# One layer of a neighbourhood-attention, retention and gated-MLP network on one core: sums of activation blocks by adding DMA transfers, and four edits to the order of weights, stores and finishes

## The chip, the core and the metric

The kernel runs on one core of one Trainium2 chip. A core has five engines with an instruction queue each: TensorE (PE in the profile, its weight loads PEld), VectorE (DVE), ScalarE (ACT), GpSimd (POOL) and SyncE (SP), which here only issues DMA transfers. SyncE, ScalarE and GpSimd have DMA queues of their own (SPq, ACTq, POOLq in the profile). The metric is the time of one launch in microseconds on the device, as the median of several runs.

## The reference

One layer over 1024 latent tokens of width 1024 on a grid of 16 x 64, with 256 context tokens, in fp32. Cut to what matters:

```python
hx = modulate(rmsnorm(x), sh1, sc1);  hc = modulate(rmsnorm(ctx), csh1, csc1)
q, k, v, rq, rk, rv, rg, ga, gb = split(hx @ w_in)        # and the same of hc
o_na  = neighbourhood_attention(q, k, v, context keys and values)    # 8 heads of 64
o_ret = layernorm(bidirectional_retention(rope(rq), rope(rk), rv)) * silu(rg)   # 4 heads, 128 -> 256
x = x + g1 * ((sigmoid(ga) * (o_na @ w_proj_na) + sigmoid(gb) * (o_ret @ w_proj_ret)) @ w_out)
h = modulate(rmsnorm(x), sh2, sc2)
u = conv3(h @ w_up) + conv_b                              # depthwise over tokens, d_ff = 2816
a, val = split(u)
x = x + g2 * ((silu(a) * val) @ w_down)
return rmsnorm(x) * final_g
```

## The kernel before

**Products.** Every fp32 product is made of three TensorE passes on a reduced fp32 type. Each operand is split in a high part, a copy by ScalarE (L88), and a low part, the source minus the high part by VectorE (L89); the passes are high x high, high x low and low x high. So each loaded block passes one ScalarE and one VectorE instruction before TensorE can use it.

**Buffers of weights.** A weight block of 128 x 512 is loaded by SyncE's queue into a tile `raw` (three buffers, L93), and split into a tile of the common ring `wc` (`wtile()`, six buffers) or into a tile that the caller gives (`wload(..., into=t)`).

**Stages in the order of time.** Start (to about 98 us); neighbourhood attention with gate projections between its parts (to about 388); the four retention heads (to about 670); remaining gate projections (to about 721); the attention projection and the gates that use seven products for eight blocks (to about 1035); the output projection (to about 1130); the up stage with the convolution (to about 1543); the down stage (to about 1756); the last finishes.

**Retention.** `Head` (L1114) loads eight weight blocks of a head by key block kb. Blocks from KH = 4 on go into tiles `wx`, six buffers in the pool `rt` of this stage; blocks 0 to 3 go into the common ring. `front(i)` computes a chunk's projections from all eight blocks; the first two chunks are context (L123 to L125 with `hc`), the next ones latent (`hx`). `decay_masks` builds the decay tables from a table `dtab` loaded at L1104, on ScalarE (L1108, L1109) and VectorE. The computation of a chunk's output (`Mix`) follows one head later; `mix_c` (L1244 on) transposes an output block, copies it by ScalarE and stores it to `d_oret` by ScalarE's queue. For the last two blocks of the last head the copy goes into a tile `oe` in a `raw` buffer, the store is put in a list `stores`, and SyncE issues it after the attention rows have been loaded (L1383, L1384).

**Attention projection.** The attention rows `onr` are loaded, transposed in groups of four into six PSUM banks (`tpn`, L1388), and split from PSUM by ScalarE (L1390) and VectorE (L1391) into `ona`. Then come the products `pn`, each with a weight block `w_pna[db, 0]` (L1520).

**Up stage.** `Seven` (L1398) computes a 2 x 2 block product by seven products (Strassen in Winograd's form). Its sums of weights s1 to s4 are POOL instructions (L1405 to L1408). `Up.step(n)` does product n of one unit; 22 units run interleaved, about 19.7 us each. When all four results of a unit are there, `conv` (L1781) filters gate and value on ScalarE and VectorE (L1786 to L1788) and multiplies them (L1790) into `at`, whose two halves are the blocks A11, A21 (j below NH = 11) or A12, A22 (its partner j + NH). The units are ordered j, j + NH, j + 1, and so on, so every second unit completes a pair. Then `conv` stores A12 and A22, makes S1 = A21 - A22, S2 = S1 - A11, S3 = A11 - A21, S4 = A12 + S2 on POOL (L1804) in `raw` buffers, and stores each by SyncE, all in the DRAM tensor `d_a`.

**Sums by transfers.** Sums of weight blocks for the down stage are made in DRAM: `block_sums` (L549) copies blocks and adds others onto them by POOL-issued DMA transfers with an accumulating operation. `puts(it, src, n)` (L583) first copies a column of `src` on POOL, which makes POOL wait until `src` is written, and then issues the next n of these transfers. In the up stage this happens at products 1 and 3 of each unit after the first; what is left of the list is issued behind the last unit.

**Who sets the order.** A scheduler of the framework orders each engine's instructions by its own estimates. `late` (L536) pins an instruction behind everything written before it on its engine; it is used for the adding transfers. Inside `manual_schedule` the written order holds; the last four-pair block loop of the down stage (L2002 on) is such a region.

**Down stage.** `steps(p, ...)` (L1917 on) runs step p of seven: for each of 11 pairs j, `operands` takes the activation block and weight block named in `DOWN[p]` from a stream of loads that runs ahead (`ur`, twelve buffers), splits both (`ahl`, `wc`), and 12 matmuls add them to four banks, one for each of QB = 4 token blocks. Between the steps the banks are combined: `p1` (step 0), `u2` (L1959, step 1), `u3` (step 3), and so on. `finish(tb, dh)` (L1940 on) makes the final norm of a token block: two short POOL instructions for the root (L1942, L1943), one scaling each on ScalarE (L1945) and VectorE (L1946), two stores by SyncE.

```python
DOWN = (("A11", "B11"), ("S2", "T2"), ("A12", "B21"), ("S3", "T3"), ("S1", "T1"), ("A22", "T4"), ("S4", "B22"))
```

Of the kernel before, what the change touches and what calls it, by code (L numbers as in the profile page):

```python
# [8 lines left out]
F32 = mybir.dt.float32  # L9
F32R = mybir.dt.float32r  # L10
# [30 lines left out]
def tile_hybrid_layer(ctx, tc: tile.TileContext, io, dbg=None):  # L41
# [1072 lines left out]
    class Head:  # L1114
        def __init__(self, h):
            self.h = h
            fwd = h % 2 == 0
            self.order = list(range(NTB)) if fwd else list(range(NTB - 1, -1, -1))
            self.back = self.order[::-1]
            self.ci = 0 if fwd else 1  # L1120
            self.oi = 1 - self.ci
            self.wr = []
            for kb in range(KB):
                t = rt.tile([P, 2, 512], F32R, tag="wx", bufs=6, name="wx") if kb >= KH else None
                self.wr.append(wload(io["w_ret"][h, kb], into=t))
# [118 lines left out]
        def mix_c(self, n):  # L1244
# [4 lines left out]
            h = self.h  # L1249
            end = h == RH - 1 and n >= NTB - 2  # L1250
            if end:
                ot = wpool.tile([P, 512], F32, tag="raw", bufs=3, name="oe")[:, : 2 * P].rearrange("p (b t) -> p b t", b=2)
            else:
                ot = rt.tile([P, 2, P], F32, tag="ot", bufs=2, name="ot")
            act.copy(ot, tp)
            stores.append((d_oret[2 * h : 2 * h + 2, :, tb * P : (tb + 1) * P].rearrange("b p t -> p b t"), ot))
            if not end:
                act.dma_start(*stores.pop())

    stores = []  # L1260

# [73 lines left out]
    while not mix.done():  # L1335
        slot(pieces_of(tl, 2 if mix.n < NTB else 3), mix)
    for it in (tl, gate_sums):
        for _ in it:
            pass
# [39 lines left out]
    for n in range(KB):  # L1379
        raw = g_raw("onr")  # L1380
        sync.dma_start(raw, d_onat[n * P : (n + 1) * P])
        onr.append(raw)
    while stores:  # L1383
        sync.dma_start(*stores.pop(0))  # L1384
    for n, raw in enumerate(onr):
# [130 lines left out]
    for db in range(KB):  # L1516
        if db % 2 == 0:
            hs = hx_sums(db // 2)
            next(hs)
        wp = [wload(io["w_pna"][db, 0])]  # L1520
        for half in range(2):
# [256 lines left out]

    acts = {}

    def conv(j, gate, value):  # L1781
# [7 lines left out]
        act.activation(ta, ta, AF.Silu)  # L1789
        vec.tensor_tensor(at, ta, at, ALU.mult)  # L1790
        acts[j] = (at[:, 0:512], at[:, 512:1024])
        if j < NH:
            sync.dma_start(d_a[A11, j], acts[j][0])
            return

        j -= NH
        (a11, a21), (a12, a22) = acts[j], acts[j + NH]
        sync.dma_start(d_a[A12, j], a12)
        sync.dma_start(d_a[A22, j], a22)
        prev = {}  # L1800
        for c, x, y, o in ((S1, a21, a22, ALU.subtract), (S2, S1, a11, ALU.subtract), (S3, a11, a21, ALU.subtract), (S4, a12, S2, ALU.add)):
            x, y = (prev[v] if isinstance(v, int) else v for v in (x, y))
            prev[c] = wpool.tile([P, 512], F32, tag="raw", bufs=3, name="sa")
            pool.tensor_tensor(prev[c], x, y, o)  # L1804
            sync.dma_start(d_a[c, j], prev[c])

# [74 lines left out]
    for i, n in interleaved(PLAIN, NF):  # L1881
        units[i].step(n)
        if n in (1, 3) and i > PLAIN:
            puts(dn_sums, (units[i].u2 if n == 1 else units[i].u3)[:, 0:1], 2)
    for _ in dn_sums:
        pass
    pu[1].release()
    pu[0].release()
# [17 lines left out]
    def operands(p, j):  # L1906
        a, w = h2p.tile([P, 2, 512], F32R, tag="h2", bufs=KB, name="ahl"), wtile()
        for t, c in zip((a, w), DOWN[p]):
            split(t[:, 0], t[:, 1], stream.get((j, c)))
        return a, w  # L1910
# [45 lines left out]

    steps(1, range(NH), True, False)
    for b in range(QB):
        vec.tensor_tensor(u2[b], banks[1][b], p1[b], ALU.add)  # L1959

# [39 lines left out]
    with tc.manual_schedule():  # L2000
        for b in range(QB):
            ts = slice(b * P, (b + 1) * P)  # L2002
            for i, (a, w) in enumerate(tl):
                open3(banks[0][b], a[:, 0, ts], a[:, 1, ts], w[:, 0], w[:, 1], False, i == NL - 1)
            z, junk = dw_tile("z", 4), dw_tile("xr", 4)
# [117 lines left out]
```

## Time and profile before

| | |
|---|---|
| time, median of 3 runs | 1763.56 us (1763.47 to 1765.64) |
| the profiled execution's own time | 1766.17 us |
| its span, first to last instruction | 1764.4 us |
| TensorE / VectorE / ScalarE / POOL busy | 98% / 71% / 48% / 33% of the span |
| DMA queues of SyncE / POOL | 38.3% / 14.1% of 16 engines' span |
| ur<-d_a loads (activation blocks of the down stage) | 77 of 256 KB, 5.3 us median to landing |
| d_a<-at and d_a<-sa stores | 33 and 44 of 256 KB, 2.7 and 2.1 us median |

How to read it: a line of a group or of a timeline names the source line, the engine, the operation, output and input tiles, and the shape; behind it stand the start and duration, or the busy time and the mean. Brackets hold the idle time of that engine just before the instruction and what ended it. TensorE's matmuls are pipelined: a row of 0.39 us is issued every 0.23 us or so.

### The profile page before, as it was taken

Reading aid. Unit: us, or ns where it says so; the run is one execution under the profiler, and the core shown is the slowest. Engines: PE = TensorE matmul, PEld = TensorE weight load, DVE = VectorE, ACT = ScalarE, POOL = GpSimd, SP = SyncE. Lnnn points to the kernel's source line nnn. Section 1 sums busy time; section 2 is a strip of 40 time slices with the busy share of each in tenths; the row PEclk is TensorE's granted clock in tenths of the full one; section 3 lists DMA queues with packets and bytes.
Section 4 is the critical chain, followed back from the end, with each engine's and each line's share of the span. In section 5 each row is a group of like instructions: output and inputs, shape, how many; then the busy total and the mean of one; then the engine's idle time right before and its main releaser. Section 6 shows DMA issues by size and latency. Waiting matters only on the chain.

```text
span 1764.4 us, 25076 instructions
## 1 busy us (share of the span) xinstructions
PE 1729.5 (98%) x8405; PEld 1429.3 (81%) x8405; DVE 1246.0 (71%) x2454; ACT 849.9 (48%) x1826; POOL 575.1 (33%) x703
## 2 busy tenths in 40 slices
PE   8999999999999999999999999999999999999997
PEld 4688888878888888788888888788888877888886
DVE  4777787754676666765554657877999988866655
ACT  5666666652443534443444323544444444544443
POOL 1000001001343444513222211023677776431444
PEclk9999999999999999999999999999999999999999
DMA  9154445542222313568876566766445554797753
GB/s 345 62 163 145 125 151 169 153 113 53 78 75 60 88 40 92 169 239 270 264 231 239 195 195 193 255 212 200 141 137 166 163 164 140 227 294 271 242 171 143
DMA packets 139249, 301.49 MB, mean 171 GB/s; under 512 B 18320, under 2 KB 30768, under 8 KB 134320
## 3 DMA queue, kind: packets, MB, share of 16 engines
q1 hardware_dynamic: 117584, 230.93, 38.3%
q0 software_dynamic: 9920, 58.73, 14.1%
q10 hardware_dynamic: 11616, 10.23, 1.7%
q8 instruction: 66, 1.08, 0.2%
q14 instruction: 63, 0.52, 0.1%
HBM read 239.25 MB, written 110.38 MB: 198 GB/s over the span
## 4 chain that ended last, share of the span: by engine, by line
PE 48%; issue 6%; DVE 6%; POOL 4%; DMA 3%; ACT 2%; SPq 0%; POOLq 0%; ACTq 0%; DVEq 0%
PE u L1396 26%; DMA ur<-d_a 2%; PE pr L114 2%; PE pr L113 2%; PE pr L112 2%; PE mm L125 1%; PE mm L123 1%; PE mm L124 1%; PE om L124 1%; PE om L125 1%; PE om L123 1%; DVE wc L89 1%; PE pn L114 1%; PE y L1396 1%; PE pn L113 1%
## 5 line engine op out<-in xcount | busy, mean ns | idle before, releaser
L1396 PE MATMUL u<-T,wc 128*128 128x512 f32 x960 | 225.4, 390 | 0.7 <-ACT pu L1430 0.3
L1396 PE MATMUL y<-wc,ahl 128*128 128x512 f32 x924 | 212.3, 391 | 2.5 <-DVE wc L89 1.8
L1396 PEld LDWEIGHTS u<-T,wc 128*128 128x128 f32 x960 | 179.3, 188 | 41.4 <-ACT pu L1430 4.3
L1396 PEld LDWEIGHTS y<-wc,ahl 128*128 128x128 f32 x924 | 174.5, 189 | 40.0 <-DVE wc L89 2.5
L89 DVE TENSOR_TENSOR wc<-ur,wc 128x512 fp32r<-128x512 f32 x161 | 140.8, 878 | 52.3 <-ACT wc L88 52.1
L88 ACT CAST wc<-ur 128x512 fp32r<-128x512 f32 x161 | 99.8, 621 | 132.3 <-PE u L1396 71.0
L113 PE MATMUL mm<-low,wc 128*128 128x512 f32 (+1 forms) x328 | 124.1, 378 | 0.0
L1396 PE MATMUL u<-h2a,wc 128*128 128x512 f32 x480 | 113.2, 390 | 2.7 <-DVE pu L1439 2.7
L1396 PEld LDWEIGHTS u<-h2a,wc 128*128 128x128 f32 x480 | 89.8, 188 | 22.9 <-issue 3.2
L112 PE MATMUL mm<-hx,wc 128*128 128x512 f32 x264 | 107.5, 407 | 0.2 <-ACT wc L635 0.2
L114 PE MATMUL mm<-hx,wc 128*128 128x512 f32 x264 | 105.7, 401 | 0.0
L1396 PE MATMUL u<-hxT,wc 128*128 128x512 f32 x384 | 89.6, 389 | 0.0
L584 POOL COPY pad<-st 128x1 f32<-128x1 f32 x32 | 5.9, 185 | 248.4 <-DVE st L487 248.4
L1396 PEld LDWEIGHTS u<-hxT,wc 128*128 128x128 f32 x384 | 72.1, 188 | 14.9
L89 DVE TENSOR_TENSOR ahl<-ur,ahl 128x512 fp32r<-128x512 f32 x77 | 64.1, 841 | 17.1 <-ACT ahl L88 16.6
L89 DVE TENSOR_TENSOR wc<-raw,wc 128x512 fp32r<-128x512 f32 x84 | 62.8, 753 | 18.7 <-ACT wc L88 18.7
L1804 POOL TENSOR_TENSOR sa<-at 128x512 f32<-128x512 f32 x22 | 38.7, 1758 | 102.6 <-DVE at L1790 54.0
L88 ACT CAST wc<-raw 128x512 fp32r<-128x512 f32 x84 | 51.8, 620 | 37.5 <-PE pr L114 7.6
L113 PEld LDWEIGHTS mm<-low,wc 128*128 128x128 f32 x328 | 62.1, 189 | 6.8
L88 ACT CAST wc<-s 128x512 fp32r<-128x512 f32 x56 | 34.8, 621 | 65.3 <-PE u L1396 64.9
L1182 ACT ACTIVATE kz<-r,dec 128x128 fp32r<-128x128 f32 x72 | 27.6, 401 | 79.2 <-POOL r L1163 78.7
L584 POOL COPY pad<-pu 128x1 f32<-128x1 f32 x54 | 37.4, 693 | 85.6 <-DVE pu L1433 64.7
(407 smaller groups left out, 4831.5 us busy)
## 6 DMA issues: line engine op xcount, KB each, us to landing
ur<-d_a SPq DMA_DIRECT2D x77, 256.0 KB, 5.3
ur<-in_w_up SPq DMA_DIRECT2D x74, 256.0 KB, 4.5
d_w<-in_w_down POOLq DMA_DIRECT2D x66, 256.0 KB, 6.1
aw<-in_w_ada SPq DMA_DIRECT2D x32, 512.0 KB, 4.1
d_a<-sa SPq DMA_DIRECT2D x44, 256.0 KB, 2.1
ur<-d_w SPq DMA_DIRECT2D x44, 256.0 KB, 3.4
d_s<-in_w_up POOLq DMA_DIRECT2D x36, 256.0 KB, 6.0
d_a<-at SPq DMA_DIRECT2D x33, 256.0 KB, 2.7
```

The costliest lines, as they stand in the source:

```text
L88: act.copy(hi, src)
L89: (lo_eng or vec).tensor_tensor(lo, src, hi.bitcast(F32), ALU.subtract)
L112: pe.matmul(out, wh, xh, start=k == 0, stop=False)
L113: pe.matmul(out, wh, xl, start=False, stop=False)
L114: pe.matmul(out, wl, xh, start=False, stop=k == n - 1)
L123: pe.matmul(out, ah, bh, start=first, stop=False)
L124: pe.matmul(out, ah, bl, start=False, stop=False)
L125: pe.matmul(out, al, bh, start=False, stop=last)
L584: late(pool.tensor_copy(tick, src))
L1182: act.activation(kz[:, d, 0], k, AF.Copy, scale=self.dec(d))
L1396: pe.matmul(out, a, b, start=first and n == 0, stop=last and n == 2, skip_group_check=True)
L1804: pool.tensor_tensor(prev[c], x, y, o)
```

## The change

Four edits.

1. Head 0 puts its weight blocks 4 and 5 into the common ring as well; only blocks 6 and 7 go into `wx`.
2. The last two retention output blocks are stored like all others, from `ot` by ScalarE's queue; the list `stores` goes. The first two weight blocks of the attention projection are loaded and split (`wpn`) ahead of the remaining gate projections instead of in the projection's loop.
3. `conv` makes no sums on POOL. For j below NH it stores A11, and A11 and A21 again into the places of S2, S1 and S3. For the partner it negates `at` in the product itself and stores -A22, -A12 and -A12 again into the place of S4. Four accumulating POOL transfers per pair then form S3 += A11, S1 += A22, S2 += S1, S4 += S2 in DRAM, one at each `puts` of the up stage, the rest behind the weight sums. So the signs of some blocks change: A12 is negated again where it is split, and the down stage's combinations subtract where they added. Step 1 closes its bank and step 3 starts a new one; the scaling of rows (L1974, L1975) works in `p1` instead of `u2`.
4. In step 5 the last two of the four finishes are moved behind the first token block's matmuls of the last region; `z` has six buffers instead of four.

```diff
-                t = rt.tile([P, 2, 512], F32R, tag="wx", bufs=6, name="wx") if kb >= KH else None
+                t = rt.tile([P, 2, 512], F32R, tag="wx", bufs=6, name="wx") if kb >= (KH if h else 6) else None
...
-            end = h == RH - 1 and n >= NTB - 2
-            if end:
-                ot = wpool.tile([P, 512], F32, tag="raw", bufs=3, name="oe")[:, : 2 * P].rearrange("p (b t) -> p b t", b=2)
-            else:
-                ot = rt.tile([P, 2, P], F32, tag="ot", bufs=2, name="ot")
+            ot = rt.tile([P, 2, P], F32, tag="ot", bufs=2, name="ot")
             act.copy(ot, tp)
-            stores.append((d_oret[2 * h : 2 * h + 2, :, tb * P : (tb + 1) * P].rearrange("b p t -> p b t"), ot))
-            if not end:
-                act.dma_start(*stores.pop())
+            act.dma_start(d_oret[2 * h : 2 * h + 2, :, tb * P : (tb + 1) * P].rearrange("b p t -> p b t"), ot)
...
+    wpn = [wload(io["w_pna"][db, 0]) for db in range(2)]
     for it in (tl, gate_sums):
...
-    while stores:
-        sync.dma_start(*stores.pop(0))
...
-        wp = [wload(io["w_pna"][db, 0])]
+        wp = [wpn[db] if db < 2 else wload(io["w_pna"][db, 0])]
...
-        vec.tensor_tensor(at, ta, at, ALU.mult)
-        acts[j] = (at[:, 0:512], at[:, 512:1024])
+        lo, hi = at[:, 0:512], at[:, 512:1024]
         if j < NH:
-            sync.dma_start(d_a[A11, j], acts[j][0])
+            vec.tensor_tensor(at, ta, at, ALU.mult)
+            for c, t in ((A11, lo), (S3, hi), (S1, hi), (S2, lo)):
+                sync.dma_start(d_a[c, j], t)
             return
-
+        vec.scalar_tensor_tensor(at, ta, -1.0, at, ALU.mult, ALU.mult)
         j -= NH
-        (a11, a21), (a12, a22) = acts[j], acts[j + NH]
-        sync.dma_start(d_a[A12, j], a12)
-        sync.dma_start(d_a[A22, j], a22)
-        prev = {}
-        for c, x, y, o in ((S1, a21, a22, ALU.subtract), (S2, S1, a11, ALU.subtract), (S3, a11, a21, ALU.subtract), (S4, a12, S2, ALU.add)):
-            x, y = (prev[v] if isinstance(v, int) else v for v in (x, y))
-            prev[c] = wpool.tile([P, 512], F32, tag="raw", bufs=3, name="sa")
-            pool.tensor_tensor(prev[c], x, y, o)
-            sync.dma_start(d_a[c, j], prev[c])
+        for c, t in ((A22, hi), (A12, lo), (S4, lo)):
+            sync.dma_start(d_a[c, j], t)
+        act_sums.extend((c, y, j) for c, y in ((S3, A11), (S1, A22), (S2, S1), (S4, S2)))
+
+    act_sums = []
+
+    def act_sum(n):
+        for c, y, j in act_sums[:n]:
+            late(pool.dma_start(d_a[c, j], d_a[y, j], accum_op=ALU.add, max_dma_last_dim=8192))
+        del act_sums[:n]
...
             puts(dn_sums, (units[i].u2 if n == 1 else units[i].u3)[:, 0:1], 2)
+            act_sum(1)
     for _ in dn_sums:
         pass
+    act_sum(len(act_sums))
...
-            split(t[:, 0], t[:, 1], stream.get((j, c)))
+            src = stream.get((j, c))
+            if c == "A12":
+                act.activation(t[:, 0], src, AF.Copy, scale=-1.0)
+                vec.scalar_tensor_tensor(t[:, 1], src, -1.0, t[:, 0].bitcast(F32), ALU.mult, ALU.subtract)
+            else:
+                split(t[:, 0], t[:, 1], src)
...
-    steps(1, range(NH), True, False)
+    steps(1, range(NH), True, True)
     for b in range(QB):
-        vec.tensor_tensor(u2[b], banks[1][b], p1[b], ALU.add)
+        vec.tensor_tensor(u2[b], banks[1][b], p1[b], ALU.subtract)
...
-    steps(3, range(NH), False, False)
+    steps(3, range(NH), True, False)
     for b in range(QB):
-        vec.tensor_tensor(u3[b], banks[1][b], p1[b], ALU.add)
+        vec.tensor_tensor(u3[b], u2[b], banks[1][b], ALU.subtract)
     for b in range(QB):
-        pool.tensor_tensor(u2[b], u2[b], gate2[:, gs(1)], ALU.mult)
-        pool.tensor_tensor(u2[b], rows_of(b, 1), u2[b], ALU.subtract)
+        pool.tensor_tensor(p1[b], u2[b], gate2[:, gs(1)], ALU.mult)
+        pool.tensor_tensor(p1[b], p1[b], rows_of(b, 1), ALU.add)
...
-        x, z = rows_of(tb, 0), dw_tile("z", 4)
+        x, z = rows_of(tb, 0), dw_tile("z", 6)
         part[tb, 0] = z
-        vec.tensor_tensor(z, banks[1][b], p1[b], ALU.add)
+        vec.tensor_tensor(z, u2[b], banks[1][b], ALU.subtract)
...
-        finish(tb, 0)
+        if b < QB - 2:
+            finish(tb, 0)
...
+            if b == 0:
+                for tb in (NTB - 2, NTB - 1):
+                    finish(tb, 0)
...
-            vec.tensor_tensor(z, z, u2[b], ALU.add)
+            vec.tensor_tensor(z, p1[b], z, ALU.subtract)
```

More of the change, by code (lines that the diff above doesn't have):

```diff
@@ L1249, in mix_c @@
             h = self.h
-            end = h == RH - 1 and n >= NTB - 2
-            if end:
-                ot = wpool.tile([P, 512], F32, tag="raw", bufs=3, name="oe")[:, : 2 * P].rearrange("p (b t) -> p b t", b=2)
-            else:
-                ot = rt.tile([P, 2, P], F32, tag="ot", bufs=2, name="ot")
+            ot = rt.tile([P, 2, P], F32, tag="ot", bufs=2, name="ot")
             act.copy(ot, tp)
-            stores.append((d_oret[2 * h : 2 * h + 2, :, tb * P : (tb + 1) * P].rearrange("b p t -> p b t"), ot))
-            if not end:
-                act.dma_start(*stores.pop())
-    stores = []
+            act.dma_start(d_oret[2 * h : 2 * h + 2, :, tb * P : (tb + 1) * P].rearrange("b p t -> p b t"), ot)
     class Mix:
@@ L1777, in get @@
             return self.tiles[n]
-    acts = {}
     def conv(j, gate, value):
@@ L2004, in tile_hybrid_layer @@
                 open3(banks[0][b], a[:, 0, ts], a[:, 1, ts], w[:, 0], w[:, 1], False, i == NL - 1)
-            z, junk = dw_tile("z", 4), dw_tile("xr", 4)
+            if b == 0:
+                for tb in (NTB - 2, NTB - 1):
+                    finish(tb, 0)
+            z, junk = dw_tile("z", 6), dw_tile("xr", 4)
             part[b, 1] = z
             vec.tensor_tensor(z, banks[0][b], gate2[:, gs(1)], ALU.mult)
-            vec.tensor_tensor(z, z, u2[b], ALU.add)
+            vec.tensor_tensor(z, p1[b], z, ALU.subtract)
             square(b, 1, junk)
```

## The prediction, on record before the result

> **What bounds the kernel now.** I read the page's busy shares first, then the waits of TensorE, then the timeline around each of those waits. The first two lines are of the page, the rest of the view of waits (what TensorE waited for: us in total, times, longest).
>
> ```profile
> PE 1729.5 (98%) x8405; PEld 1429.3 (81%) x8405; DVE 1246.0 (71%) x2454; ACT 849.9 (48%) x1826; POOL 575.1 (33%) x703
> core 0: 1764.4 us, clock 0.994
> ...
> PE tp L279 <- ACT ccol L241: 4.5, 1, 4.5
> ...
> PE mm L123 <- ACT wx L88: 3.2, 2, 2.7
> PE u L1396 <- DVE pu L1439: 2.7, 4, 0.8
> ...
> PE tpn L1388 <- DVE ona L1391: 2.1, 1, 2.1
> ```
>
> TensorE is busy for 1729.5 of 1764.4 us at a clock of 0.994. No matmul is added or removed, so all that can be won lies in the other 35 us, and all that can be lost is a new wait of TensorE. The start (the first of these waits) and the end are untouched. The diff touches the other three rows shown, and one place in the last stage: four places, taken in the order of time. In between TensorE is never late, so 575 us of POOL or 850 us of ScalarE work cost nothing there.
>
> **First head's weights (key blocks 4, 5 into the common ring).** Timelines of TensorE, ScalarE and SyncE's queue; each row is start, duration, instruction, and in brackets the idle time before it and what ended it.
>
> ```profile
> 388.56 0.62 PE L123 MATMUL mm<-wx,hc 128*128 128x384 f32 x2 [0.52 <-ACT wx L88]
> 395.03 0.62 PE L123 MATMUL mm<-wx,hc 128*128 128x384 f32 x2 [2.68 <-ACT wx L88]
> 398.16 0.80 PE L123 MATMUL mm<-wc,hx 128*128 128x512 f32 x1 [1.44 <-ACT r L1153]
> ...
> 381.33 0.59 ACT L362 COPY gs<-mm 128x512 f32<-128x512 f32 x1 [0.89 <-PE mm L114]
> 387.90 1.65 ACT L88 CAST wx<-raw 128x512 fp32r<-128x512 f32 x3
> 392.67 0.40 ACT L1108 ACTIVATE e<-dtab,lg 128x128 f32<-128x128 f32 x1 [3.13 <-DMA dtab<-in_dtab]
> 394.36 0.62 ACT L88 CAST wx<-raw 128x512 fp32r<-128x512 f32 x1 [0.70 <-DMA raw<-in_w_ret]
> ```
>
> The `wx` tiles are in the pool of the retention stage, so their splits start at 387.90. Block 7's raw load needs one of three raw buffers, which those splits free; it lands so late that it is split at 394.36, and TensorE waits 0.52 + 2.68 + 1.44 = 4.64 us. The common ring exists earlier: the gate matmuls that read it last end at about 381.3 (the copy of their sum at 381.33), so blocks 4 and 5 can be split then, two raw buffers come free, and block 7 lands before 388. The first two waits, 3.2 us, should go. The third stays in part: ScalarE stands in order behind the table wait to 392.67, and after it come the decay tables and the copies that free the banks. If the scheduler leaves that order as it is, only the late split and its wait (0.62 + 0.70 us) go from the chain, a gain of 1.3; if it puts the copies first, all of 4.6. I take 3.0, nearer to the 3.2 of the two `wx` waits.
>
> It has a cost: head 0 now fills the six common slots, so head 1's first blocks sit in the raw buffers until head 0's last matmuls. Rows of ScalarE and TensorE at the change of heads:
>
> ```profile
> 451.96 0.62 ACT L88 CAST wx<-raw 128x512 fp32r<-128x512 f32 x1 [0.73 <-DMA raw<-in_w_ret]
> ...
> 456.69 0.34 PE L123 MATMUL mm<-wx,hc 128*128 128x384 f32 x1
> ```
>
> Now the last block of head 1 is split by 452.6 and used at 456.69: 4.1 us in hand. Later loads (five instead of three behind the freeing, some 1 to 1.4 us apart) would bring it to about 458.6. That is 0 (other work fills it) to 2 us; I take 0.5. The other heads keep their pattern. Net 2.5.
>
> **Last retention rows and the first two weights behind them.** TensorE, ScalarE, VectorE, queues of SyncE and ScalarE:
>
> ```profile
> 721.60 2.78 PE L1388 MATMUL tpn<-ident,onr 128*128 128x128 f32 x24
> 726.47 1.25 PE L1388 MATMUL tpn<-ident,onr 128*128 128x128 f32 x8 [2.09 <-DVE ona L1391]
> ...
> 724.21 0.62 ACT L88 CAST wc<-raw 128x512 fp32r<-128x512 f32 x1 [0.79 <-DMA raw<-in_w_pna]
> 724.73 4.00 ACT L1390 CAST ona<-tpn 128x512 fp32r<-128x512 f32 x8
> ...
> 725.74 4.86 DVE L1391 TENSOR_TENSOR ona<-tpn,ona 128x512 fp32r<-128x512 f32 x8
> ...
> 721.27 3.24 SPq L93 DMA_DIRECT2D raw<-in_w_pna  x3
> ...
> 722.41 0.34 ACTq L363 DMA_DIRECT2D d_gate<-gs  x1
> ```
>
> Six banks hold the transposes; the seventh group of four waits until ScalarE and VectorE have split the first. ScalarE splits a weight first (724.21, itself waiting for a late load), because the last store stands ahead of the load on SyncE and holds a raw buffer. With these two weights loaded before the last gates are computed (raw buffers and ring slots are free in that stretch), ScalarE can begin the eight copies at about 722.4, when its gate store is out, and VectorE at 723.1 instead of 725.74. The first bank is free 2.6 us sooner than at 726.4: the wait of 2.09 goes, and the first product behind it needs no weight. I take 2.2, from 1.5 (the loads are late again and half is left) to 3.4 (the 0.79 us and a split more). The two stores by ScalarE cost about 0.34 us of issue each, on an engine idle there; if that cover were gone, 0.7 us. The `ot` buffer's reader lands before anything reuses it.
>
> **Block sums by adding transfers.** Rows of TensorE, VectorE, the page's group, POOL, and the DMA issues (count, size, median us to landing):
>
> ```profile
> 1417.25 3.00 PE L1396 MATMUL u<-h2a,wc 128*128 128x512 f32 x12 [0.63 <-DVE pu L1439]
> ...
> 1394.76 1.28 DVE L1787 SCALAR_TENSOR_TENSOR ta<-uu,cw,ta 128x1023 f32<-128x1023 f32 x1
> 1414.26 2.24 DVE L1787 SCALAR_TENSOR_TENSOR ta<-uu,cw,ta 128x1023 f32<-128x1023 f32 x1 [0.28 <-ACT ta L1786]
> ...
> L1804 POOL TENSOR_TENSOR sa<-at 128x512 f32<-128x512 f32 x22 | 38.7, 1758 | 102.6 <-DVE at L1790 54.0
> ...
> 1408.06 0.79 POOL L552 DMA_DIRECT2D d_w<-d_w  x1
> 1409.26 2.09 POOL L552 DMA_DIRECT2D d_w<-in_w_down  x1
> ...
> d_w<-d_w POOLq DMA_DIRECT2D x22, 256.0 KB, 5.6
> ```
>
> TensorE waits four times, 2.7 us, for VectorE's `pu`, each time in a unit that completes a pair. There VectorE's filter step took 2.24 us, while the same step took 1.28 in the unit before. What differs is POOL: four sums (1.76 us in the mean) stand ahead of its weight sums and push them onto VectorE's step. After the change POOL issues four adding transfers per pair (44 in all) of about 0.8 us instead, spread over slots 8 to 11 us apart, and does not wait in order for VectorE's product (54 us in ten waits now). So 0.96 us per pair of VectorE's delay may go, more than the wait of 0.63. Between 0 (the weight sums, earlier by what POOL gained, meet another VectorE step) and 2.7 I take 2.2, near the row. VectorE's product becomes a three-operand form, which by the row at 1394.76 is no dearer. SyncE's stores stay at 77.
>
> At 5.6 us, each sum's predecessor has landed before the next slot. It is at the end, after the last unit, that this breaks: see the second rival. The forecast costs it at nothing.
>
> **Order of the last finishes.** TensorE and ScalarE:
>
> ```profile
> 1738.88 0.49 PE L1396 MATMUL y<-wc,ahl 128*128 128x512 f32 x1 [0.73 <-ACT wc L88]
> 1740.76 1.43 PE L1396 MATMUL y<-wc,ahl 128*128 128x512 f32 x5 [1.39 <-DVE wc L89]
> ...
> 1737.62 0.61 ACT L1933 ACTIVATE xr<-z 128x512 f32<-128x512 f32 x1
> 1738.23 0.60 ACT L88 CAST wc<-ur 128x512 fp32r<-128x512 f32 x1
> ```
>
> ScalarE reaches a weight's split only at 1738.23, and VectorE is held the same way by a finishing product that waits for POOL's root. With the last two finishes behind block 0's matmuls, the split is due about 1.1 us sooner, VectorE's half soon after, and 0.73 + 1.39 = 2.1 us go. The moved work (per finish two short POOL operations, one pass on ScalarE, one on VectorE, two stores) lies beside some 4 us of matmuls of block 0; uncovered it would cost about 1.5 us. I take 2.1, from 0 to 2.5. The sign changes and the row scalings replace instructions one for one; in step 5 `u2` takes the place of `p1` and is ready far earlier. Nothing.
>
> **Sum.** 2.5 + 2.2 + 2.2 + 2.1 = 9.0 us. It is worked out on an execution of 1766.17 us (span 1764.4), 0.15% above the median of 1763.56; taken off the median it gives 1754.5 us.
>
> **Rivals.** First, the waits only move: the tables still hold ScalarE (1.3), head 1 pays 2, the `pu` wait stays, half of the last place goes, 1.5 at the retention rows; 1.3 - 2 + 1.5 + 0 + 1.1 = 1.9, giving 1761.7. For it speaks that each of these waits has a next one close behind. Second, on the slower side, the end of the last pair's sums. POOL, the windows view (the columns are length, then busy time of PE, PEld, DVE, ACT and POOL, clock, DMA share, GB/s), the first VectorE read of step 1's banks, and the chain:
>
> ```profile
> 1551.71 1.67 POOL L1804 TENSOR_TENSOR sa<-at 128x512 f32<-128x512 f32 x1 [14.84 <-DVE at L1790]
> 1583.09 0.77 POOL L552 DMA_DIRECT2D d_w<-d_w  x1 [7.32 <-DMA d_w<-d_w]
> ...
> 1560.00:1600.00 40.00, 40.00 (x178) 33.11 (x178) 20.71 (x32) 19.08 (x34) 8.84 (x13) 1.00 1.00 315
> ...
> 1600.05 2.47 DVE L1959 TENSOR_TENSOR pd<-y,pd 128x512 f32<-128x512 f32 x4
> ...
> 1562.16 12.82 DMA ur<-d_a
> ```
>
> Now the twelve last weight sums leave POOL from 1560 to 1583, because POOL waits 14.84 us for VectorE. Without that wait they can leave from about 1537 to 1560, and six activation sums follow, which wait on each other's landing: with 7.3 to 8.9 us each, the one that step 1's last pair loads has landed by about 1585, its load and split take some 7 us, and TensorE wants it at about 1599 (1.4 us ahead of the read at 1600.05). That leaves 7 us. If the weight sums leave as late as now (1583), the sum issues at about 1601, lands at 1609, is split at 1616, and TensorE waits 17 us: 1754.5 + 17 = 1771.5, slower by 8. It decides from 7 us of delay. The transfers are saturated here (share 1.00, a load of 12.82 us). [...] Third, plain starvation there: the added transfers delay a load past its cover, 1 to 5 us back, about 1758. Fourth, the change does not do what it says: block 7 and the two weights still load late, so 2.2 + 2.1 = 4.3 are left, 1759.3.
>
> **How the numbers follow.** What a measurement of this kernel can tell from no change is about 0.2%, 3.5 us: faster is below 1760.0, slower above 1767.1. Forecast (1750.4 to 1757.5, the upper bounds being 4.6 + 3.4 + 2.7 + 2.5 = 13.2) 0.55; waits that move 0.18, within 0.2%; late last sums 0.10, slower; starvation 0.12 and not done 0.05, both still faster. Faster 0.72, same 0.18, slower 0.10. The range runs from 1750.4 to 1763.0, the first rival with a further us lost; the late sums are left out.
>
> **What would show it.** Right: no `wx` wait at 388 to 398, a third `tpn` group without a break, no `pu` rows from 1400 to 1540, no break between 1737 and 1742, and TensorE unbroken from 1545 to 1700. Wrong: a wait of TensorE behind `ahl` near 1600, POOL held by a `d_a` landing ahead of its weight sums, a `wx` wait near 456, or the wait behind `r` near 398 grown to more than 3 us.

## The result and the profile after

The kernel after takes 1753.34 us in the median (1752.38 to 1753.98), the kernel before, run beside it, 1764.3 us (1763.47 to 1765.64). The ratio is 0.9937, 95% interval 0.9919 to 0.9954: 11.1 us less, between 8.1 and 14.3. The forecast was 1754.5, which is 9.0 us less.

The page of the kernel after, its busy shares and its span:

```profile
PE 1724.2 (98%) x8405; PEld 1426.8 (81%) x8405; DVE 1224.6 (70%) x2454; ACT 852.3 (49%) x1826; POOL 537.6 (31%) x703
core 0: 1751.7 us, clock 0.996
```

TensorE has the same 8405 matmuls and is busy for 5.3 us less; the span is 12.7 us shorter, so its idle time fell by 7.4 us. What TensorE waited for (us in total, times, longest); line numbers behind L1250 are 9 to 11 lower than before, so L1387 is the matmul of L1396:

```profile
PE tp L279 <- ACT ccol L241: 4.5, 1, 4.5
...
PE y L1387 <- DVE wc L89: 2.1, 2, 1.7
...
PE dS L125 <- DVE kz L1183: 1.3, 2, 0.9
PE mm L123 <- ACT r L1153: 0.6, 1, 0.6
...
PE tpn L1379 <- DVE ona L1382: 0.5, 1, 0.5
```

No row of `wx` L88 behind ScalarE is left (3.2 us before), and none of `pu` behind VectorE (2.7 us before). The transposes' wait went from 2.1 to 0.5, the wait behind `r` from 1.4 to 0.6. Two rows speak against the forecast: `kz` is new, and of the 2.1 us near 1740 there is still a wait of 1.7. The timelines show the places. TensorE and ScalarE at the first head:

```profile
391.40 0.52 PE L123 MATMUL mm<-wx,hc 128*128 128x384 f32 x2
394.31 0.50 PE L123 MATMUL mm<-wc,hx 128*128 128x512 f32 x1 [0.63 <-ACT r L1153]
...
385.31 0.61 ACT L88 CAST wc<-raw 128x512 fp32r<-128x512 f32 x1
389.33 1.13 ACT L88 CAST wx<-raw 128x512 fp32r<-128x512 f32 x2
393.98 0.27 ACT L1153 COPY r<-mm 128x128 f32<-128x128 f32 x1
394.18 0.40 ACT L1108 ACTIVATE e<-dtab,lg 128x128 f32<-128x128 f32 x1
```

Both `wx` splits are done before 390.5, and the scheduler put the copy of `r` ahead of the decay tables. That is the better of the forecast's two ends. At the last matmuls, TensorE, VectorE and ScalarE:

```profile
1729.34 13.67 PE L1387 MATMUL y<-wc,ahl 128*128 128x512 f32 x59 [1.66 <-DVE wc L89]
...
1727.93 0.75 DVE L1944 SCALAR_TENSOR_TENSOR z<-z,ssf,fg 128x512 f32<-128x512 f32 x1 [0.80 <-POOL ssf L1941]
1728.60 0.69 DVE L89 TENSOR_TENSOR wc<-ur,wc 128x512 fp32r<-128x512 f32 x1
...
1728.49 1.34 ACT L1943 ACTIVATE x<-x,ssf 128x512 f32<-128x512 f32 x2
1729.73 0.61 ACT L88 CAST wc<-ur 128x512 fp32r<-128x512 f32 x1
```

The moved finishes are written behind block 0's matmuls, but nothing makes their instructions wait for these matmuls. On VectorE the finish at 1727.93 stands ahead of the split that TensorE waits for, and on ScalarE two stand ahead of the last splits.

The windows view adds what no wait row tells: the granted clock (the columns are the stretch and its length, busy time of PE, PEld, DVE, ACT and POOL, clock, DMA share, GB/s). Before:

```profile
98.00:102.00 4.00, 4.00 (x31) 3.82 (x30) 2.15 (x5) 2.87 (x6) 0.00 (x0) 1.00 0.74 183
...
400.00:404.00 4.00, 4.00 (x14) 3.32 (x13) 1.89 (x6) 1.02 (x2) 0.00 (x0) 0.50 0.14 53
...
728.00:732.00 4.00, 3.97 (x10) 2.99 (x10) 3.23 (x6) 3.92 (x7) 4.00 (x4) 0.57 0.27 93
...
1742.00:1746.00 4.00, 4.00 (x12) 3.11 (x11) 2.92 (x5) 1.71 (x4) 0.00 (x0) 0.57 0.08 30
```

And after:

```profile
98.00:102.00 4.00, 4.00 (x29) 4.00 (x29) 1.80 (x4) 1.98 (x4) 0.00 (x0) 0.77 0.60 136
...
400.00:408.00 8.00, 8.00 (x42) 6.75 (x41) 3.88 (x14) 2.05 (x6) 1.48 (x2) 1.00 0.01 2
...
726.00:730.00 4.00, 4.00 (x19) 3.29 (x18) 3.37 (x5) 2.72 (x4) 4.00 (x4) 1.00 0.18 67
...
1733.00:1737.00 4.00, 4.00 (x20) 3.30 (x19) 1.88 (x3) 0.60 (x2) 0.00 (x0) 1.00 0.00 0
```

Before, a stretch at half clock stands behind three of the four places of the diff: 6.8 us from 397.2, 3.4 us from 728.3 and 3.4 us from 1742. After, none does, but a stretch of 3.4 us from 96.5 stands where the diff changes nothing (0.77 in the window shown). In the stretch at 0.57 from 1742 some 12 matmuls start in 4 us, in that at 1.00 from 1733 after it is 20 of the same: by these counts about 1.6 us are lost in such a stretch, an estimate.

The theories for the experiments: **theory 1**, each part gives back its own waits, as forecast; **theory 2**, a part gives more than its waits, because the clock falls behind a long wait; **theory 3**, parts gain only together or not at all.

### The profile page after: what moved, and what is told of

Same layout as the page of the kernel before. It is cut to its first block, busy times and chain, and to the rows that moved or that the text cites. A ratio compares the mean times of both kernels' runs of the same rounds, so it can differ in the third digit from the quotient of the medians.

```text
span 1751.7 us, 25084 instructions
## 1 busy us (share of the span) xinstructions
PE 1724.2 (98%) x8405; PEld 1426.8 (81%) x8405; DVE 1224.6 (70%) x2454; ACT 852.3 (49%) x1826; POOL 537.6 (31%) x703
## 4 chain that ended last, share of the span: by engine, by line
PE 50%; issue 6%; DVE 4%; DMA 4%; POOL 4%; ACT 2%; SPq 0%; POOLq 0%; ACTq 0%; DVEq 0%
PE u L1387 28%; PE pr L114 2%; PE pr L112 2%; PE pr L113 2%; DMA ur<-d_a 2%; PE mm L125 1%; PE mm L123 1%; PE mm L124 1%; PE om L125 1%; PE om L123 1%; PE om L124 1%; DMA d_a<-at 1%; PE pn L113 1%; PE pn L112 1%; PE pn L114 1%
## 5 line engine op out<-in xcount | busy, mean ns | idle before, releaser
L1387 PE MATMUL u<-T,wc 128*128 128x512 f32 x960 | 225.1, 390 | 0.5 <-ACT pu L1421 0.4
L1387 PE MATMUL y<-wc,ahl 128*128 128x512 f32 x924 | 210.4, 389 | 2.1 <-DVE wc L89 2.1
L1387 PEld LDWEIGHTS u<-T,wc 128*128 128x128 f32 x960 | 179.6, 188 | 40.1 <-ACT pu L1421 2.7
L1387 PEld LDWEIGHTS y<-wc,ahl 128*128 128x128 f32 x924 | 173.3, 188 | 38.9 <-DVE wc L89 2.9
L89 DVE TENSOR_TENSOR wc<-ur,wc 128x512 fp32r<-128x512 f32 x161 | 117.1, 730 | 60.2 <-ACT wc L88 58.3
L88 ACT CAST wc<-ur 128x512 fp32r<-128x512 f32 x161 | 99.8, 622 | 118.8 <-PE u L1387 71.4
L1387 PE MATMUL u<-h2a,wc 128*128 128x512 f32 x480 | 112.8, 390 | 0.1
L1387 PEld LDWEIGHTS u<-h2a,wc 128*128 128x128 f32 x480 | 89.9, 188 | 19.7 <-issue 0.8
L1387 PE MATMUL u<-hxT,wc 128*128 128x512 f32 x384 | 89.6, 389 | 0.0
L1387 PEld LDWEIGHTS u<-hxT,wc 128*128 128x128 f32 x384 | 72.1, 188 | 15.0
L88 ACT CAST wc<-raw 128x512 fp32r<-128x512 f32 x86 | 53.1, 623 | 39.4 <-PE u L1387 7.4
L88 ACT CAST wc<-s 128x512 fp32r<-128x512 f32 x56 | 34.9, 624 | 69.9 <-PE u L1387 67.7
L125 PE MATMUL mm<-wc,low 128*128 128x512 f32 (+1 forms) x180 | 68.5, 381 | 0.0
L1387 PE MATMUL u<-hx,wc 128*128 128x512 f32 x192 | 62.0, 390 | 0.0
```

Of the source, the lines that this page charges most:

```text
L88: act.copy(hi, src)
L89: (lo_eng or vec).tensor_tensor(lo, src, hi.bitcast(F32), ALU.subtract)
L125: pe.matmul(out, al, bh, start=False, stop=last)
L1387: pe.matmul(out, a, b, start=first and n == 0, stop=last and n == 2, skip_group_check=True)
```

## The experiments

All ratios are to the kernel before, run beside them, with 95% intervals; microseconds are the ratio times 1764.3.

**Each part alone.** The first edit:

```diff
-                t = rt.tile([P, 2, 512], F32R, tag="wx", bufs=6, name="wx") if kb >= KH else None
+                t = rt.tile([P, 2, 512], F32R, tag="wx", bufs=6, name="wx") if kb >= (KH if h else 6) else None
```

> The kernel before with only the first edit (head 0's blocks 4 and 5 in the common ring). Theory 1, each part gives its own waits back: the waits behind wx at 388 and 395 (3.2 us) are gone, the wait behind r falls from 1.4 to about 0.6, new waits of 1 to 2 us appear at the change to head 1 near 450 to 460; net 2.1 to 3.5 us, time about 0.9985 of before. Theory 2, a long wait costs more than its length because the granted clock falls behind it: the same rows, and in addition no window at about 0.5 clock after 396, so 4 to 5 us, 0.9975. Theory 3, the gain comes only together with the other edits: under 1 us.

Measured: 0.9977 (0.9965 to 0.9988), 4.1 us less (2.1 to 6.2). The `wx` rows are gone, `r` is at 0.6, and the row of `kz` appears with 1.3 as in the kernel after. One more wait of this profile:

```profile
PE tpn L1388 <- DVE ona L1391: 4.5, 1, 4.5
```

The clock is 1.00 from 392 to 408. The time is that of theory 2, but the interval takes in the whole of theory 1's range too (2.1 to 3.5). Beside it stands something that edit 1 does not touch: the transposes' wait is 4.5 us here, 2.1 in the profile before. So that wait varies, and edit 2 was sized on a small one.

The second edit alone (its lines as in the diff shown):

```diff
-            end = h == RH - 1 and n >= NTB - 2
...
+            act.dma_start(d_oret[2 * h : 2 * h + 2, :, tb * P : (tb + 1) * P].rearrange("b p t -> p b t"), ot)
+    wpn = [wload(io["w_pna"][db, 0]) for db in range(2)]
```

> The kernel before with only the second edit (last retention rows by ScalarE, two weights ahead of the last gates). Theory 1: the wait of 2.1 us of the transposes falls to about 0.5 and the 0.8 near 742 goes; 2 to 2.5 us less, 0.9987. Theory 2: in addition the window of 0.57 clock at 728 to 732 is gone; 3.5 to 4.2 us less, 0.9978. Theory 3: under 1 us.

Measured: 0.9972 (0.9957 to 0.9987), 4.9 us less (2.3 to 7.6). The transposes' wait is 0.38, the 0.8 near 742 is gone, and the clock is 1.00 from 724 to 732. Again theory 2's size, with theory 1's 0.9987 at the interval's edge.

The third edit alone:

```diff
-            pool.tensor_tensor(prev[c], x, y, o)
-            sync.dma_start(d_a[c, j], prev[c])
+        act_sums.extend((c, y, j) for c, y in ((S3, A11), (S1, A22), (S2, S1), (S4, S2)))
```

> The kernel before with only the third edit (activation sums by adding transfers, with its changes of sign). Theory 1: the four waits behind pu (2.7 us) are gone and nothing comes in the down stage; 2.2 to 2.9 us less, 0.9985. Theory 2 says the same of time, since these waits of 0.5 to 0.8 us show no lower clock. Theory 3, the transfers at the change to the down stage starve TensorE in this order: a wait of over 1 us between 1540 and 1610, and no gain.

Measured: 0.9992 (0.9983 to 1.0002), 1.4 us less (0.4 more to 3.0 less). No `pu` row behind VectorE is left, and no wait from 1540 to 1700, so theory 3's starvation is out. By time the part is not told from nothing, nor from 2.2.

The fourth edit alone:

```diff
-        finish(tb, 0)
+        if b < QB - 2:
+            finish(tb, 0)
...
+            if b == 0:
+                for tb in (NTB - 2, NTB - 1):
+                    finish(tb, 0)
```

> The kernel before with only the fourth edit (last two finishes behind the first block's matmuls, six buffers for z). Theory 1: the waits of 0.7 and 1.4 us near 1740 fall to 0 to 0.5; 1.6 to 2.1 us less, 0.999. Rival, as the profile of the whole change suggests (a wait of 1.7 us left at that place, the finishes still ahead of the last splits): 0.5 us less and one wait of 1.2 to 1.7 us left. Theory 2 adds that the clock of 0.76 to 0.82 from 1740 to 1748 goes with the waits if they fall below some length: then 1.5 us more.

Measured: 0.9993 (0.9984 to 1.0003), 1.2 us less (0.5 more to 2.8 less). TensorE and VectorE at the place:

```profile
1738.53 2.88 PE L1396 MATMUL y<-wc,ahl 128*128 128x512 f32 x7 [1.76 <-DVE wc L89]
...
1737.12 0.75 DVE L1946 SCALAR_TENSOR_TENSOR z<-z,ssf,fg 128x512 f32<-128x512 f32 x1 [0.80 <-POOL ssf L1943]
1737.79 0.68 DVE L89 TENSOR_TENSOR wc<-ur,wc 128x512 fp32r<-128x512 f32 x1
```

The rival of the expectation is right: one wait of 1.76 instead of two of 2.12. The four ratios multiply to 0.9934; the whole change measured 0.9937. The first two parts gain alone, and the four add up within their intervals, which rules theory 3 out.

**What in the second edit works.** Only its stores, the weights loaded where they were:

```diff
-                ot = wpool.tile([P, 512], F32, tag="raw", bufs=3, name="oe")[:, : 2 * P].rearrange("p (b t) -> p b t", b=2)
+            ot = rt.tile([P, 2, P], F32, tag="ot", bufs=2, name="ot")
...
-    while stores:
-        sync.dma_start(*stores.pop(0))
```

> The kernel before with only half of the second edit: the last retention rows stored from ot by ScalarE, the first two weights of the attention projection loaded where they were. If the raw buffers that the stores held were what made the weights late, the transposes' wait falls to under 1 us already. If it is the split of a weight standing ahead of the eight copies on ScalarE, 1 to 2 us are left.

Measured: 1761.4 us in one execution. The transposes, TensorE:

```profile
726.79 1.25 PE L1378 MATMUL tpn<-ident,onr 128*128 128x128 f32 x8 [0.37 <-DVE ona L1381]
```

The wait is gone with the stores alone. But the loads are early here as well: with the stores out of SyncE's queue, the scheduler put them there ahead of the attention rows.

```profile
689.82 19.71 SPq L93 DMA_DIRECT2D raw<-in_w_pna  x3
```

So the two stores were what made the weights late. Whether by the raw buffers that they held or by their place in SyncE's order this run does not tell, and it does not show what late loads would cost once the stores are gone.

**Whether POOL's sums made the `pu` waits.** The kernel after, with four POOL instructions for each pair whose results nothing uses:

```diff
+        for x, y in ((hi, lo), (lo, hi), (hi, lo), (lo, hi)):
+            pool.tensor_tensor(wpool.tile([P, 512], F32, tag="raw", bufs=3, name="sa"), x, y, ALU.subtract)
         act_sums.extend((c, y, j) for c, y in ((S3, A11), (S1, A22), (S2, S1), (S4, S2)))
```

> The kernel after, with four POOL instructions of the size of the removed sums behind each pair's product; their results are not used. If the waits behind pu came from the sums' place on POOL, four or so of 0.5 to 0.9 us come back between 1200 and 1540, 2 to 3 us in all, and the span grows by 2 to 4 us. Rival: they came from something else that the edit changed (how long the at buffers are held, the stores' order); then no pu row comes back.

Measured: 1778.21 us in one execution, span 1776.4. The waits, and then POOL at the end of the up stage:

```profile
PE u L1387 <- DVE pu L1430: 10.0, 8, 2.1
PE y L1387 <- ACT wc L88: 7.3, 1, 7.3
```

```profile
1553.83 6.77 POOL L1790 TENSOR_TENSOR sa<-at 128x512 f32<-128x512 f32 x4 [14.02 <-DVE at L1785]
...
1584.35 0.76 POOL L552 DMA_DIRECT2D d_w<-d_w  x1 [6.65 <-DMA d_w<-d_w]
...
1597.76 0.76 POOL L1797 DMA_DIRECT2D d_a<-d_a  x1 [5.45 <-DMA d_a<-d_a]
```

The `pu` waits come back, so their cause was the sums' place on POOL. They come back larger than before (10.0 against 2.7), probably since POOL now issues the adding transfers besides, which the 2 to 3 us expected left out; no run tries that. The second row was not expected at all: the last sums wait 14.02 us for VectorE, the weight sums end at 1584 as in the kernel before, the last pair's S2 is issued at 1597.76, and TensorE waits 7.3 us. That is the prediction's second rival, with its condition met by accident. Its price was too high: the sum's load followed 3.9 us behind the issue (SyncE's queue, 1601.62) and TensorE went on 3.9 us after that (1605.54), where the prediction counted 8 and 7 from an issue at 1601, so the wait is 7.3 us and not 17.

**That rival on purpose.** The kernel after, with 14 instead of 6 sums left behind the last unit:

```diff
-            act_sum(1)
+            if i < NF - 4:
+                act_sum(1)
```

> The kernel after, with no activation sums in the last four units, so that 14 instead of 6 are left behind the weight sums. This tries the prediction's rival on the slower side. If the chain on POOL waits on each landing as in the kernel after (16.9 us from one pair's S2 to the next), the S2 blocks of the last two pairs come 10 to 27 us late, TensorE waits near 1580 to 1590, and the time grows by 15 to 30 us over the kernel after. If the loads had slack enough, as the forecast's nothing would extend to, under 3 us.

Measured: 1773.13 us in one execution, 19.8 more than the median of the kernel after. TensorE, POOL and SyncE's queue:

```profile
1588.56 5.76 PE L1387 MATMUL y<-wc,ahl 128*128 128x512 f32 x12 [8.17 <-ACT wc L88]
1602.21 4.16 PE L1387 MATMUL y<-wc,ahl 128*128 128x512 f32 x8 [7.90 <-ACT wc L88]
...
1580.68 0.76 POOL L1795 DMA_DIRECT2D d_a<-d_a  x1 [7.17 <-DMA d_a<-d_a]
1594.43 0.76 POOL L1795 DMA_DIRECT2D d_a<-d_a  x1 [7.22 <-DMA d_a<-d_a]
...
1584.64 0.32 SPq L1753 DMA_DIRECT2D ur<-d_a  x1
1585.06 0.37 SPq L1753 DMA_DIRECT2D ur<-d_w  x1
```

POOL stands 7.2 us for a landing ahead of each of these two issues, SyncE stands behind POOL (its load of the sum at 1584.64 comes as the sum lands), and the next weight's load stands behind that in SyncE's order. So the row of waits names ScalarE's split of a weight, although it is the activation sum that is late. The clock in the three windows of 10 us from 1580 to 1610 is 0.61 to 0.69, and TensorE is busy for 5.7 us longer than in the kernel after (1729.9 against 1724.2), beside 16.1 us of these waits.

**Is the clock's part real.** The kernel before, with TensorE kept at work where it waits for the transposes:

```diff
-        for k in range(NPAIR):
-            pe.transpose(tp[:, k], raw[:, k * P : (k + 1) * P], ident)
+        for _ in range(6 if n == 5 else 1):
+            for k in range(NPAIR):
+                pe.transpose(tp[:, k], raw[:, k * P : (k + 1) * P], ident)
```

> The kernel before, with the four transposes of the sixth attention row group issued six times instead of once, into the same bank with the same values: 20 transposes more, about 2.3 us of TensorE work in a place where it waits 2.1 to 4.5 us anyway. Theory 2 (the clock falls behind a long wait and the slow windows cost about as much again): the wait shrinks by about 2 us, no window of half clock at 724 to 732, and the kernel with more work takes 1.5 to 3 us less than the kernel before (0.9985). Theory 1 (a wait costs its length only): the work fills the wait and the time stays within 0.5 us; theory 3 (transposes do not count as activity, or they delay the split of the sixth group): the slow window stays, time 0 to 2 us more.

Measured: 1.0007 (0.9993 to 1.002). TensorE, then the window behind:

```profile
722.07 4.96 PE L1389 MATMUL tpn<-ident,onr 128*128 128x128 f32 x44
728.18 1.25 PE L1389 MATMUL tpn<-ident,onr 128*128 128x128 f32 x8 [1.15 <-DVE ona L1392]
```

```profile
730.00:734.00 4.00, 4.00 (x18) 3.31 (x19) 4.00 (x7) 3.97 (x8) 4.00 (x3) 1.00 0.01 2
```

The work fits into the wait and the slow window is gone, as theory 2 has it, but the time does not fall: 0.9985 is outside the interval. As theory 1 says, the filled wait is free. In this profile `pu` waited 3.9 us instead of 2.7 and the weight near 742 1.1 instead of 0.8, which would hide 1.5 us in one execution, but not in a median of ten. So by the median, the time of the window does not come back. In the stretch itself it does. From the first of these transposes to the first `tpa` behind the attention projection (774.34 in the kernel before) TensorE has the same matmuls in every kernel, here with 20 more. Before, after and this run:

```profile
721.60:774.34 52.74, 49.81 (x226) 40.55 (x224) 42.91 (x61) 30.39 (x54) 20.67 (x14) 0.97 0.66 223
...
719.14:767.64 48.50, 47.97 (x226) 39.43 (x224) 40.12 (x56) 27.70 (x48) 19.91 (x14) 1.00 0.58 192
...
722.07:774.87 52.80, 50.45 (x245) 41.54 (x244) 43.23 (x61) 30.41 (x54) 20.68 (x14) 1.00 0.68 218
```

Less the 2.18 us of the added transposes (4.96 against 2.78), TensorE is busy for 48.3 us here: that is the 48.0 of the kernel after and not the 49.8 of the kernel before. Edits 1, 3 and 4 alone have 50.4, 49.3 and 50.2 at clocks of 0.94 to 0.97. So a slow window costs 1.4 to 2.5 us here, and filling the wait gives it back; in the whole kernel that is about the noise, since this run's interval reaches 1.2 us less.

**Two mends.** The finishes written behind block 0's combination, so that VectorE and ScalarE do reach them after the last splits:

```diff
-            if b == 0:
-                for tb in (NTB - 2, NTB - 1):
-                    finish(tb, 0)
             z, junk = dw_tile("z", 6), dw_tile("xr", 4)
...
             square(b, 1, junk)
+            if b == 0:
+                for tb in (NTB - 2, NTB - 1):
+                    finish(tb, 0)
```

> The kernel after, with the two moved finishes written behind the first block's combination in the ordered region, so that ScalarE and VectorE reach them after the last splits. In the kernel after they still stand ahead of the last splits, and a wait of 1.7 us is left. Theory 1: that wait falls below 0.5, the rest is the same; 1.2 to 1.7 us less than the kernel after, 0.9928 of before. Rival: the wait belongs to the splits' own loads and stays, no change. Rival on the slow side: the finishes now delay the last blocks' combinations and the end grows by 0.5 to 1.5 us.

Measured: 0.9922 (0.9907 to 0.9937), 1750.98 us. TensorE's last matmuls now begin with a wait of 0.16 instead of 1.66:

```profile
1727.07 13.65 PE L1387 MATMUL y<-wc,ahl 128*128 128x512 f32 x59 [0.16 <-DVE wc L89]
```

Theory 1 of this expectation is right by the row; by time it is not told from the kernel after, whose interval it overlaps. And one block of head 0 in the common ring instead of two:

```diff
-                t = rt.tile([P, 2, 512], F32R, tag="wx", bufs=6, name="wx") if kb >= (KH if h else 6) else None
+                t = rt.tile([P, 2, 512], F32R, tag="wx", bufs=6, name="wx") if kb >= (KH if h else 5) else None
```

> The kernel after, with only block 4 of head 0 in the common ring instead of 4 and 5; blocks 5, 6 and 7 fit the three raw buffers. If it is the third raw buffer for block 7 that decides, the wx waits at 388 to 396 stay away as with two blocks. The waits at the change to head 1 (1.5 us in the kernel after) shrink to under 1 us, because one ring slot is free for head 1. Time 0 to 1.5 us less than the kernel after. Rival: ScalarE has one split more at 388, the wait behind it (0.5 us) comes back and the table order costs 1 us: 1 us more.

Measured: 0.9927 (0.991 to 0.9943), 1751.57 us. No `wx` row and no `kz` row is left; `r` waits 1.2 instead of 0.6. Three raw buffers hold three blocks, so one block in the ring is enough, and by the rows the second only cost head 1 its early loads; by time this one too overlaps the kernel after. Both together:

> The kernel after with both mends: one block of head 0 in the common ring instead of two, and the two moved finishes behind the first block's combination. If both gains are independent: no waits behind kz near 450 to 460, none over 0.5 us near 1727; 2.5 to 4 us less than the kernel after, about 1750 us or 0.9915 of before. Rival: the mends overlap with variation of the clock windows, and it is no better than each alone (0.9925).

Measured: 1748.25 us, 0.9889 (0.9869 to 0.9909), below the interval of the kernel after. It beats both kernels: the one before by 19.6 us, the one after by 5 us by the medians and 8.5 us by the ratios. That is more than the 2.4 and 1.8 us of the two mends alone. Part of it may be chance: the wait near 95, which no edit touches, is 0.4 us in this profile and 2.1 in that of the kernel after.

## Why the prediction was right, point by point

- **First head.** The mechanism held: blocks 4 and 5 free two raw buffers, block 7 is early, 3.2 us of waits go, and the third falls from 1.44 to 0.63, so 4.0 instead of the 3.0 taken. The cost at head 1 was found, but mis-sized: 0.5 was taken, the rows show 1.5 (1.3 behind `kz`, 0.2 behind a `wx` split). Net 2.5 both ways of counting; measured 4.1, with 2.5 inside the interval. A stretch of half clock behind the wait went too, which the sum did not have. From the first matmul on `hc` to the first transpose of `onr` TensorE has the same matmuls; before and after:

```profile
381.92:721.60 339.68, 334.39 (x1752) 285.84 (x1751) 212.64 (x717) 138.39 (x394) 118.66 (x194) 0.99 0.29 76
...
383.35:719.14 335.79, 332.43 (x1752) 283.86 (x1751) 216.56 (x721) 140.87 (x398) 119.54 (x195) 1.00 0.31 81
```

Of the 3.9 us, 2.0 are busy time. The six profiles without this edit take 339.2 to 341.7 us here, the five with it 334.7 to 336.4, and the two with one block in the ring 333.4 and 333.8.
- **Last retention rows.** Forecast 2.2, measured 4.9 (2.3 to 7.6), the term most undersized. The 2.09 of the profile before was a small one: where this part was not changed, 4.5 (edit 1 alone), 3.4 (edit 3 alone) and 3.3 us (edit 4 alone) were waited. One execution gave the size of a wait that hangs on when a load lands. The sum also left out the 0.8 us near 742 and the slow window: the stretch up to `tpa` takes 52.7 to 55.6 us in these four profiles and 48.4 to 48.5 with this part. Of the two changes of this part the stores' was enough; with them gone the loads came early by themselves.
- **Sums by transfers.** The reason given, POOL's place pushing onto VectorE, is shown by the sums put back. The 2.2 taken agree with the rows: in the six profiles with POOL's sums the `pu` waits behind VectorE come to 0.7 to 3.9 us, 2.2 in the mean, and with the transfers to 0.3 at most (the dummy sums aside). The time alone, 1.4 (0.4 more to 3.0 less), can't confirm them. Two steps of the reason were wrong. "At 5.6 us, each sum's predecessor has landed before the next slot": in seven units of the up stage POOL stood 0.6 to 6.5 us for a landing. And the filter step named for the wait is not quicker: it takes 1.48 us in the mean instead of 1.42, and still over 2.2 in three units. VectorE, kernel before and after:

```profile
1410.51 1.78 DVE L89 TENSOR_TENSOR wc<-ur,wc 128x512 fp32r<-128x512 f32 x1
...
1422.75 0.69 DVE L89 TENSOR_TENSOR wc<-ur,wc 128x512 fp32r<-128x512 f32 x1
1425.73 2.24 DVE L1776 SCALAR_TENSOR_TENSOR ta<-uu,cw,ta 128x1023 f32<-128x1023 f32 x1 [0.67 <-ACT ta L1775]
```

VectorE comes to the step about 1 us earlier (0.45 us ahead of TensorE's `h2a` matmuls at 1426.18; before, 0.52 us behind those at 1413.74): steps ahead of it, like this split, take less time, and TensorE does not wait. The fourth wait, at 1534, does not fit the reason either: its filter step takes 1.28 us, and the long one is the first filter step of that unit (2.31 us, beside POOL's last sum). And the product's three-operand form is dearer: 1.91 us in the mean, where the two-operand form took 1.42 before and takes 1.72 beside it now.
- **Order of the finishes.** The step that failed: "With the last two finishes behind block 0's matmuls, the split is due about 1.1 us sooner". Written behind is not queued behind: 0.46 of the 2.1 us went. The moved instructions wait for nothing of block 0, so they were queued ahead of the last splits. Written behind something that does wait for block 0, they gave the rest of the row; by time that gain is not told from nothing.
- **The rivals.** The first, waits that only move, is out by its size (1761.7), though two of its items came in part: head 1 paid 1.5, and in the last place a wait of 1.66 was left. The second, late last sums, did not come. The kernel after's POOL and SyncE's queue, and the window:

```profile
1552.54 0.76 POOL L552 DMA_DIRECT2D d_w<-d_w  x1 [8.70 <-DMA d_w<-d_w]
1569.89 0.76 POOL L1795 DMA_DIRECT2D d_a<-d_a  x1 [6.75 <-DMA d_a<-d_a]
...
1575.84 0.32 SPq L1753 DMA_DIRECT2D ur<-d_a  x1
```

```profile
1530.00:1600.00 70.00, 70.00 (x310) 57.95 (x310) 42.52 (x59) 34.79 (x59) 17.38 (x20) 1.00 1.00 314
```

The weight sums have left by 1553 (forecast: about 1560), the last S2 has landed by 1576 (about 1585), TensorE is unbroken, and the transfers fill 1.00 of the engines. Where its condition was met as stated, in the run with the dummy sums, the price was a wait of 7.3 us and not 17. The 16.1 us of waits with 14 sums left are of two pairs, so that they lie near 17 is chance. The third rival, starvation, did not come: TensorE has no wait from 1530 to 1600. Nor did the fourth: block 7 and the two weights are early. No issue of an adding transfer of `d_a` was as long as the 2.09 us at 1409.26 in the kernel before: the last ones took 0.76 to 1.05 us, and three in a row 2.34 together, and all 44 took 0.76 to 1.50 us each.
- **The total** came out near the forecast by errors that offset each other: two terms too small (4.1 and 4.9 for 2.5 and 2.2), two too large (1.4 and 1.2 for 2.2 and 2.1). One more was luck: the sum has 9.0 us of waits and nothing for the clock, while in the two profiles 7.4 us of the 12.7 are waits and 5.3 are the same matmuls at a higher clock.

## What to carry to other kernels

An instruction that is written later is later only if it waits for something there; look at the queue of its engine, not at the program, before you take a wait as gone (here 1.66 us were left, and 0.16 once the finishes waited for block 0). Where a ring of three buffers was filled by four early loads, moving one block elsewhere was enough here, and the second one was paid by the next user (1.3 us behind `kz`). A wait that ends with a load's landing should be sized from several executions: the same place waited 2.1 to 4.5 us in kernels that do not differ there. And where the granted clock falls behind a wait, its row is not the whole price (1.4 to 2.5 us more of busy time behind the transposes here): take the time of the same matmuls from one fixed place to another, and the busy time in it.

## What the runs showed of the hardware

In these profiles TensorE's granted clock fell to 0.5 for 3.4 us (from 728.3 in the kernel before), 6.8 us (from 397.2 there) or 10.2 us (from 1583.9 with 14 sums left) behind waits of 2.1 us and more, and behind some shorter ones (0.73 and 1.39 us close together near 1740 in the kernel before, 1.76 in the fourth edit alone), though not each time: behind the same wait of 2.0 to 2.1 us near 95 the clock was 1.00 in the kernel before and 0.5 for 3.4 us in the kernel after, and behind the 1.66 us at 1729 it was 1.00. The length of the wait alone does not decide: in the kernel before, the transposes' wait of 2.09 us was followed by 0.57 from 728 to 732, and the 2.0 us near 95 by 1.00. What wait it takes stays open. The adding transfers in the kernel after (count, size, median us to landing):

```profile
d_a<-d_a POOLq DMA_DIRECT2D x44, 256.0 KB, 7.5
```

They take 7.5 us in the median, not the 5.6 of the weight sums on which the forecast rested, so most of a slot of 8 us; and POOL's waits for landings, in order (8.70 us at 1552.54, 6.75 at 1569.89), are what set the margin at the end.
